# MoE of a two-layer block: the backs and gathers placed by two pairs of experts, and one small tile widened

## The chip, the cores and the metric

The kernel runs on one NeuronCore of one Trainium2 chip, as one program. The metric is the device time of one execution in microseconds (us), less is better; beside it stands one execution taken by the hardware profiler. Of the core's engines PE is the matrix engine (PEld its weight loads), DVE the vector engine, ACT the scalar engine, POOL GpSimd and SP the queue that issues most DMAs. All DMAs run on 16 DMA engines.

## The reference

Two blocks follow each other on 256 tokens of width 1024. The change touches only the mixture of experts (MoE) that stands twice in the second block, once in each layer, with 16 experts of inner width 512, two per token:

```python
def routed_moe(x, router_w, router_b, w_gate, w_up, w_down):
    xt = x.reshape(B * S, D)
    aff = jax.nn.sigmoid((xt @ router_w).astype(jnp.float32))
    sel = aff + router_b.astype(jnp.float32)
    # the best of 4 groups of 4 experts, and in it the 2 best experts
    ...
    w = jnp.take_along_axis(aff, e_idx, axis=1)
    w = w / jnp.sum(w, axis=-1, keepdims=True)
    gates = jnp.einsum('nk,nke->ne', w, jax.nn.one_hot(e_idx, N_EXPERTS, dtype=jnp.float32)).astype(x.dtype)
    y = jnp.zeros_like(xt)
    for e in range(N_EXPERTS):
        h = jax.nn.silu(xt @ w_gate[e]) * (xt @ w_up[e])
        y = y + gates[:, e:e + 1] * (h @ w_down[e])
    return y.reshape(B, S, D)
```

All of it is float32. The weights of one MoE layer are 96 pieces of 1 MB.

## The kernel before

`moe` (from line 1071) computes one MoE layer. Each expert has room for `CAP` = 64 tokens, so two experts (a pair) fill the 128 partitions, and there are `NP` = 8 pairs. A 0/1 matrix `Dg` says which token stands in which place of which expert (`places`). Four steps use it:

- `gather(q, xr)` brings the tokens of four experts (two pairs) into their places: for each of eight blocks of 128 columns four matmuls of `xr`, the high and the low half of the tokens, with `Dg` (line 1123), and an ACT eviction into `xg[q]` (line 1125). `gather(0)` stands ahead of the experts.
- `back` makes what leads back. Sixteen small matmuls (line 1132) take the gates to the places, two DVE copies put them into `gs` (lines 1134, 1135); sixteen transposes (line 1140) turn `Dg`, four ACT copies put them into `DT` (line 1142).
- `pair_in(load, j, between)` does the gate (tag A) and up (tag B) products of pair `j`, 32 matmuls `pe` (line 1154) with the two experts side by side in the array, calls `between()` after tag A, and multiplies `silu`, `gs` and the up product (line 1164).
- `flip` transposes the result (line 1170); `pair_out` does the down products `yp` (line 1185), splits them, and adds them to `x` through `DT` with the matmuls `psc` (lines 1197 to 1199).

`experts` runs `pair_in(j)`, `pair_out(j-1)`, `flip(j)` for the eight pairs. A float32 matmul stands in the trace as two instructions. The order on each engine is made by the framework's planner from this order and its own costs, so small steps are found mixed with `pe`.

The weights come through `Loads`: 96 loads of 1 MB in a fixed order on SP, which takes its DMAs in order. Each goes into a slot; `take` hands a loaded slot to the matmuls and `give` puts it back, upon which the next load is issued. The slots are opened in steps: M1 and M2 (5 together), three that are used once, M3 (6, not filled again from load 84 on), and M4 (2). M4 lies where `xr` and the router's tiles lay, so `room_left` opens it after the last gather. Two loads are issued as it opens.

`between` before: pair 0 `back` and `counts`, pair 1 `gather(1)`, pair 2 `gather(2)`, `gather(3)` and `room_left`. The counts tell whether an expert has more than 64 tokens; a loop that handles such a case (line 1350 on) follows each layer and is not entered here.

The pool `sp` holds small tiles for the whole program. Its tile `mr` is 128 x 1; a tile takes at least 32 bytes of a partition, and there are two buffers.

Of the kernel before, what the change touches and what calls it, by code (L numbers as in the profile page):

```python
# [7 lines left out]
F32 = mybir.dt.float32  # L8
# [7 lines left out]
P = 128  # L16
T = 256
NT = T // P
D = 1024
# [6 lines left out]
CAP, NP = 64, 8  # L26
# [42 lines left out]
class Net:  # L69
# [1016 lines left out]
    def moe(self, x, l, mp, load, early, mixed, probe, ahead):  # L1086
# [6 lines left out]
        nc, A, tc = self.nc, self.A, self.tc  # L1093
        v, mm = nc.vector, nc.tensor.matmul
        with ExitStack() as ctx:
            room, op = (ctx.enter_context(tc.tile_pool(name=n, bufs=1, reuse_waits="tile")) for n in ("m2", "mo"))
            gates, mask = (op.tile([P, NT, 16], F32, name=n) for n in ("gates", "mask"))
            Dg = op.tile([P, NT, 16 * CAP], F32R, name="Dg")
            DT = op.tile([P, NP, T], F32R, name="DT")
            gs, r = op.tile([P, NP], F32, name="gs"), op.tile([P, NT, 16], F32, name="r")  # L1100
# [14 lines left out]
            def gather(q, xr, tags="D"):  # L1115

                xg[q] = zone[q // 2][:, q % 2].rearrange("p (k n) -> p k n", k=KD)
                for k in range(KD):
                    if k % 2 == 0:
                        pg = self.bank(tags, "pg")  # L1120
                    ps = pg[:, T * (k % 2):T * (k % 2) + T]
                    for n, (t, a) in enumerate((t, a) for t in range(NT) for a in xr):
                        mm(ps, a[:, t, P * k:P * k + P], Dg[:, t, T * q:T * q + T], start=(n == 0),
                           stop=(n == 2 * NT - 1))
                    nc.scalar.activation(xg[q][:, k], ps, AF.Identity, bias=sh[:, k:k + 1], scale=sc[:, k:k + 1])

            def back():

                pg = self.bank("D", "pgs")
                for j in range(NP):  # L1130
                    for t in range(NT):
                        mm(pg[:, 2 * j:2 * j + 2], Dg[:, t, P * j:P * j + P].bitcast(F32), gates[:, t, 2 * j:2 * j + 2],
                           start=(t == 0), stop=(t == NT - 1))
                v.tensor_copy(gs[0:64], pg[0:64, 0:16:2])
                v.tensor_copy(gs[64:128], pg[64:128, 1:16:2])
                for j in range(0, NP, 2):
                    ps = self.bank("D", "pdt")
                    for i in range(2):
                        for t in range(NT):
                            nc.tensor.transpose(ps[:, T * i + P * t:T * i + P * t + P],  # L1140
                                                Dg[:, t, P * (j + i):P * (j + i) + P].bitcast(F32), self.ident)
                    nc.scalar.copy(DT[:, j:j + 2], ps.rearrange("p (i n) -> p i n", i=2))

            def pair_in(load, j, between=lambda: None):

                pss = []
                for tag in "AB":
                    ps = self.bank(tag, "pe")
                    for c in range(2):
                        ws = [load.take() for _ in range(2)]  # L1150
                        for k in range(4):
                            for e, (w, _) in enumerate(ws):
                                b = CAP * e
                                mm(ps[b:b + CAP], xg[j // 2][:, 4 * c + k, P * (j % 2) + b:P * (j % 2) + b + CAP],  # L1154
                                   w[:, 512 * k:512 * k + 512], start=(c == 0 and k == 0), stop=(c == 1 and k == 3),
                                   tile_position=(0, b))
                        for w in ws:
                            load.give(w)
                    pss.append(ps)
                    if tag == "A":  # L1160
                        between()
                sg = sp.tile([P, 512], F32, name="sg")
                nc.scalar.activation(sg, pss[0], AF.Silu)
                v.scalar_tensor_tensor(sg, sg, gs[:, j:j + 1], pss[1], ALU.mult, ALU.mult)  # L1164
                return sg

            def flip(sg):
                pt = self.bank("D", "pt")
                for i in range(4):
                    nc.tensor.transpose(pt[:, P * i:P * i + P], sg[:, P * i:P * i + P], self.ident)  # L1170
                hT = sp.tile([P, 4, P], F32, name="hT")
                nc.scalar.copy(hT, pt.rearrange("p (i m) -> p i m", i=4))
                return hT
# [29 lines left out]
            def experts(load, first, after):  # L1203
                prev = None
                for j in range(NP):
                    sg = pair_in(load, j, after.get(j, lambda: None))
                    if prev is not None:
                        pair_out(load, *prev)
                    prev = (j, flip(sg), ALPHA if first and j == 0 else 1.0)
                pair_out(load, *prev)  # L1210

            with ExitStack() as rt:
                rp = rt.enter_context(tc.tile_pool(name="rt", bufs=1))
                f = lambda name, shape: rp.tile(shape, F32, name=name)
                xr = [rp.tile([P, NT, D], F32R, name=n) for n in ("xrh", "xrl")]
# [8 lines left out]
                ps = self.bank("A", "cs2")  # L1224
# [6 lines left out]
                def scored(t, y):  # L1231

                    lt = lg[:, 16 * t:16 * t + 16]

                    def logits(n):
                        ps = self.bank("BD"[t], "ptr")
                        for q in range(4):
                            k = 4 * n + q
                            nc.tensor.transpose(ps[:, P * q:P * q + P], x[:, t, P * k:P * k + P], self.ident)
                        xT = rp.tile([P, 4, P], F32, name="xT", tag="xT", bufs=2)  # L1240
                        nc.scalar.copy(xT, ps.rearrange("p (q m) -> p q m", q=4))
                        for q in range(4):
                            k = 4 * n + q
                            mm(lt, xT[:, q], w2[:, 0, k], start=(k == 0), stop=(k == KD - 1))
                    self.summed(x, t, y, logits)
                    m, rs = self.moments(t)
                    z, mr = self.sp.tile([P, 16], F32, name="z", tag="z"), self.sp.tile([P, 1], F32, name="mr", tag="mr")
                    v.tensor_scalar(mr, m, rs, -1.0, ALU.mult, ALU.mult)
                    v.scalar_tensor_tensor(z, cs2[:, 0], mr, cs2[:, 1], ALU.mult, ALU.add)
                    v.scalar_tensor_tensor(z, lt, rs, z, ALU.mult, ALU.add)  # L1250
                    nc.scalar.activation(aff[:, t], z, AF.Sigmoid)
                    box.append(v.tensor_scalar(xn[t], x[:, t], m, rs, ALU.subtract, ALU.mult).ins)
# [77 lines left out]
                def counts():  # L1330
                    cn = self.bank("D", "cn")
                    mm(cn[:, 0:16], self.ones, mask[:, 0], start=True, stop=False)
                    mm(cn[:, 0:16], self.ones, mask[:, 1], start=False, stop=True)
                    v.tensor_reduce(of[:, 0:1], cn[0:1, 0:16], AX.X, ALU.max)
                    v.tensor_scalar(of[:, 1:2], of[:, 0:1], float(CAP), None, ALU.is_gt)
                    v.tensor_copy(over, of[:, 1:2])
# [3 lines left out]
                def room_left():  # L1340
                    rt.close()
                    load.open(rt.enter_context(tc.tile_pool(name="m4", bufs=1, reuse_waits="tile")), M4)
                experts(load, True, {0: lambda: (back(), counts()), 1: lambda: gather(1, xr),
                                     2: lambda: (gather(2, xr), gather(3, xr), room_left())})
            more.close()
            self.open_weights()
            first = ahead()
# [2 lines left out]
            with tc.If(left > 0):  # L1350
                with tc.tile_pool(name="r2", bufs=1) as rp:
                    xr = [rp.tile([P, NT, D], F32R, name=n) for n in ("xrh", "xrl")]
                    with tc.For_i(0, T // CAP - 1, 1):
                        for t in range(NT):
                            self.split(xr[0][:, t], xr[1][:, t], xn[t])
                        v.tensor_scalar(r, r, float(-CAP), None, ALU.add)
                        for q in range(4):
                            places(q)
                            gather(q, xr)
                        back()  # L1360
                        load = self.expert_loads(l)
                        load.open(early, M1[l])
                        load.open(room, M2[l])
                        experts(load, False, {})
        return gb, first

    def expert_loads(self, l):
# [397 lines left out]
```

## Time and profile before

| | us |
|---|---|
| median of the runs shown (3) | 2248.41 |
| lowest and highest | 2245.25, 2248.60 |
| profiled execution, its own time | 2246.95 |
| profiled execution, its span | 2244.80 |
| DVE busy in it | 1285.5 |
| ACT busy in it | 836.4 |
| PE busy in it | 2103.6 |

The span is the time between the first and the last instruction of the program in the trace; the execution's own time has some 2 us around it. PE busy counts pipelined matmuls with modelled ends, so a busy PE may still be waiting for its weights in part. The granted clock is that of the matrix engine: 1.00 is 2.4 GHz and 0.50 is 1.2 GHz. In the trace the first MoE layer lies between about 1577 and 1831 us, the second between about 1979 and 2233 us.

### The profile page before, as it was taken

How to read it: one execution, taken by the hardware profiler on the slowest of the kernel's cores; microseconds unless marked ns; L12 is line 12 of the kernel's file. 1: busy time of each engine (PE TensorE's matmuls, PEld its weight loads, DVE VectorE, ACT ScalarE, POOL GpSimd, SP SyncE). 2: the span in 40 equal slices, each digit the busy share in tenths (PEclk: the TensorE clock that was granted, in tenths of full speed). 3: DMA queues.
4: the chain of work that ended last, by engine and by line, in shares of the span. 5: the costliest groups of instructions: out<-in, count | busy, mean ns of one | idle time of the engine just before them, and what ended most of it. 6: DMA issues, size and time to landing. Idle time of an engine off the chain costs nothing. (4 is left out here: it accounts for less than half of the span.)

```text
span 2244.8 us, 30723 instructions
## 1 busy us (share of the span) xinstructions
PE 2103.6 (94%) x12156; PEld 1598.4 (71%) x12156; DVE 1285.5 (57%) x2572; ACT 836.4 (37%) x1467; POOL 65.8 (3%) x76
## 2 busy tenths in 40 slices
PE   7999999999989998999999999899999968989996
PEld 5878887886879997899897999787443338644332
DVE  5897637645578768776685655667211157641213
ACT  3222325435455444444554544364220015522000
POOL 0000000102000000000000000200000021100000
PEclk9999999999999999999999999999899989989998
DMA  8567634433248875785346554433789956278996
GB/s 322 201 239 274 242 113 152 128 117 48 76 169 311 289 267 199 283 290 204 132 169 225 199 177 169 181 113 133 286 357 420 420 225 240 93 278 334 420 419 253
DMA packets 94747, 514.47 MB, mean 229 GB/s; under 512 B 19648, under 2 KB 21056, under 8 KB 43520
## 3 DMA queue, kind: packets, MB, share of 16 engines
q1 hardware_dynamic: 88272, 502.34, 59.9%
q10 hardware_dynamic: 5168, 5.85, 0.8%
q0 software_dynamic: 1152, 4.19, 0.6%
q8 instruction: 99, 1.62, 0.3%
q14 instruction: 56, 0.46, 0.1%
HBM read 511.30 MB, written 1.05 MB: 228 GB/s over the span
## 5 line engine op out<-in xcount | busy, mean ns | idle before, releaser
L106 DVE TENSOR_TENSOR wlo<-raw,whi 128x1024 fp32r<-128x1024 f32 x421 | 514.2, 1232 | 285.4 <-ACT whi L105 282.9
L105 ACT CAST whi<-raw 128x1024 fp32r<-128x1024 f32 x421 | 434.6, 1048 | 626.6 <-PE pa L160 186.1
L160 PE MATMUL pa<-hh,whi 128*128 128x256 f32 (+1 forms) x720 | 224.0, 311 | 4.6 <-DVE hh L285 4.6
L160 PE MATMUL pa<-hl,whi 128*128 128x256 f32 (+1 forms) x720 | 223.1, 310 | 0.6 <-DVE hl L286 0.5
L160 PE MATMUL pa<-hh,wlo 128*128 128x256 f32 (+1 forms) x720 | 222.2, 309 | 0.0
L160 PE MATMUL pb<-hh,whi 128*128 128x256 f32 (+1 forms) x720 | 221.4, 308 | 0.0
L160 PE MATMUL pb<-hh,wlo 128*128 128x256 f32 (+1 forms) x720 | 221.1, 307 | 0.0
L160 PE MATMUL pb<-hl,whi 128*128 128x256 f32 (+1 forms) x720 | 220.9, 307 | 0.0
L363 DVE SCALAR_TENSOR_TENSOR macc<-rawm,cs,macc 128x512 f32<-128x512 f32 x266 | 193.2, 749 | 13.1 <-DMA rawm<-in_w_mod 9.1
L192 PE MATMUL yacc<-whi,gh 128*128 128x512 f32 x440 | 172.8, 398 | 1.3 <-ACT gate L383 1.3
L193 PE MATMUL yacc<-wlo,gh 128*128 128x512 f32 x440 | 171.6, 393 | 0.0
L1164 DVE SCALAR_TENSOR_TENSOR sg<-sg,gs,pe 128x512 f32<-128x512 f32 x16 | 12.0, 747 | 246.8 <-PE pe L1154 246.8
L160 PEld LDWEIGHTS pa<-hh,whi 128*128 128x128 f32 x720 | 138.4, 192 | 18.1 <-DVE hh L285 5.1
L160 PEld LDWEIGHTS pa<-hl,whi 128*128 128x128 f32 x720 | 138.3, 192 | 10.4 <-DVE hl L286 1.6
L1185 PE MATMUL yp<-mw,hT 128*64 128x512 f32 x512 | 138.6, 597 | 7.5 <-DMA mw<-in_w_dn 6.2
L160 PEld LDWEIGHTS pa<-hh,wlo 128*128 128x128 f32 x720 | 138.2, 192 | 6.4
L160 PEld LDWEIGHTS pb<-hh,whi 128*128 128x128 f32 x720 | 136.7, 190 | 6.2
L160 PEld LDWEIGHTS pb<-hl,whi 128*128 128x128 f32 x720 | 136.7, 190 | 6.2
L195 PE MATMUL yacc<-whi,gl 128*128 128x512 f32 x440 | 141.0, 394 | 0.0
L160 PEld LDWEIGHTS pb<-hh,wlo 128*128 128x128 f32 x720 | 136.3, 189 | 6.2
L1154 PE MATMUL pe<-mw,xgH 128*64 128x512 f32 x512 | 122.2, 597 | 8.0 <-DMA mw<-in_w_gu 8.0
L1154 PE MATMUL pe<-mw,xgY 128*64 128x512 f32 x464 | 126.1, 608 | 0.0
(469 smaller groups left out, 3706.8 us busy)
## 6 DMA issues: line engine op xcount, KB each, us to landing
mw<-in_w_gu SPq DMA_DIRECT2D x122, 1024.0 KB, 17.2
raw<-in_ffn_w_in SPq DMA_DIRECT2D x88, 1024.0 KB, 5.0
rawm<-in_w_mod SPq DMA_DIRECT2D x72, 1024.0 KB, 5.8
mw<-in_w_dn SPq DMA_DIRECT2D x64, 1024.0 KB, 15.7
raw<-in_ffn_w_out SPq DMA_DIRECT2D x55, 1024.0 KB, 5.1
raw<-in_mix_wT SPq DMA_DIRECT2D x8, 1024.0 KB, 5.1
raw<-in_sg_wR SPq DMA_DIRECT2D x8, 1024.0 KB, 5.1
raw<-in_sg_wT SPq DMA_DIRECT2D x8, 1024.0 KB, 4.9
```

The lines of the kernel that those rows point to most:

```text
L105: self.nc.scalar.copy(hi, src)
L106: self.nc.vector.tensor_tensor(lo, src, hi.bitcast(F32), ALU.subtract)
L160: self.nc.tensor.matmul(o, w[:, k], h[:, k], start=(k == 0 and i == 0), stop=(k == nk - 1 and i == len(steps) - 1))
L192: mm(y[n], a, whi[:, cs[n]], start=first, stop=False)
L193: mm(y[n], a, wlo[:, cs[n]], start=False, stop=False)
L195: mm(y[n], b, whi[:, cs[n]], start=False, stop=last)
L363: v.scalar_tensor_tensor(o, raw[:, k], w, o, ALU.mult, ALU.add)
L1154: mm(ps[b:b + CAP], xg[j // 2][:, 4 * c + k, P * (j % 2) + b:P * (j % 2) + b + CAP], w[:, 512 * k:512 * k + 512], start=(c == 0 and k == 0 ...
L1164: v.scalar_tensor_tensor(sg, sg, gs[:, j:j + 1], pss[1], ALU.mult, ALU.mult)
L1185: mm(yp[n][b:b + CAP], hT[:, i, b:b + CAP], w[:, D * k + 512 * n:D * k + 512 * n + 512], start=(i == 0), stop=(i == 3), tile_position=(0, b))
```

## The change

`back` becomes `back(j)` and does the gates and the transposes of two pairs, j and j+1. `between` becomes one function of j: the even pairs call `back(j)` (pair 0 also `counts`), pairs 1, 3 and 5 call `gather(1)`, `gather(2)` and `gather(3)`, and `room_left` stands in pair 5, after `gather(3)`. `gather(1)` and the counts stay where they were. The loop that is not entered calls `back` in four parts. The tile `mr` is made 128 x 16, of which the first column is used; two buffers of it take 64 bytes each instead of 32.

```diff
@@ -1124,22 +1124,21 @@
                            stop=(n == 2 * NT - 1))
                     nc.scalar.activation(xg[q][:, k], ps, AF.Identity, bias=sh[:, k:k + 1], scale=sc[:, k:k + 1])
 
-            def back():
-
-                pg = self.bank("D", "pgs")
-                for j in range(NP):
+            def back(j):
+
+                pg, ps = self.bank("D", "pgs"), self.bank("D", "pdt")
+                for i in range(2):
                     for t in range(NT):
-                        mm(pg[:, 2 * j:2 * j + 2], Dg[:, t, P * j:P * j + P].bitcast(F32), gates[:, t, 2 * j:2 * j + 2],
-                           start=(t == 0), stop=(t == NT - 1))
-                v.tensor_copy(gs[0:64], pg[0:64, 0:16:2])
-                v.tensor_copy(gs[64:128], pg[64:128, 1:16:2])
-                for j in range(0, NP, 2):
-                    ps = self.bank("D", "pdt")
-                    for i in range(2):
-                        for t in range(NT):
-                            nc.tensor.transpose(ps[:, T * i + P * t:T * i + P * t + P],
-                                                Dg[:, t, P * (j + i):P * (j + i) + P].bitcast(F32), self.ident)
-                    nc.scalar.copy(DT[:, j:j + 2], ps.rearrange("p (i n) -> p i n", i=2))
+                        mm(pg[:, 2 * i:2 * i + 2], Dg[:, t, P * (j + i):P * (j + i) + P].bitcast(F32),
+                           gates[:, t, 2 * (j + i):2 * (j + i) + 2], start=(t == 0), stop=(t == NT - 1))
+                for e in range(2):
+                    b = slice(CAP * e, CAP * e + CAP)
+                    v.tensor_copy(gs[b, j:j + 2], pg[b, e:4:2])
+                for i in range(2):
+                    for t in range(NT):
+                        nc.tensor.transpose(ps[:, T * i + P * t:T * i + P * t + P],
+                                            Dg[:, t, P * (j + i):P * (j + i) + P].bitcast(F32), self.ident)
+                nc.scalar.copy(DT[:, j:j + 2], ps.rearrange("p (i n) -> p i n", i=2))
 
             def pair_in(load, j, between=lambda: None):
 
@@ -1203,7 +1202,7 @@
             def experts(load, first, after):
                 prev = None
                 for j in range(NP):
-                    sg = pair_in(load, j, after.get(j, lambda: None))
+                    sg = pair_in(load, j, lambda: after(j))
                     if prev is not None:
                         pair_out(load, *prev)
                     prev = (j, flip(sg), ALPHA if first and j == 0 else 1.0)
@@ -1244,7 +1243,7 @@
                             mm(lt, xT[:, q], w2[:, 0, k], start=(k == 0), stop=(k == KD - 1))
                     self.summed(x, t, y, logits)
                     m, rs = self.moments(t)
-                    z, mr = self.sp.tile([P, 16], F32, name="z", tag="z"), self.sp.tile([P, 1], F32, name="mr", tag="mr")
+                    z, mr = self.sp.tile([P, 16], F32, name="z", tag="z"), self.sp.tile([P, 16], F32, name="mr", tag="mr")[:, 0:1]
                     v.tensor_scalar(mr, m, rs, -1.0, ALU.mult, ALU.mult)
                     v.scalar_tensor_tensor(z, cs2[:, 0], mr, cs2[:, 1], ALU.mult, ALU.add)
                     v.scalar_tensor_tensor(z, lt, rs, z, ALU.mult, ALU.add)
@@ -1340,8 +1339,16 @@
                 def room_left():
                     rt.close()
                     load.open(rt.enter_context(tc.tile_pool(name="m4", bufs=1, reuse_waits="tile")), M4)
-                experts(load, True, {0: lambda: (back(), counts()), 1: lambda: gather(1, xr),
-                                     2: lambda: (gather(2, xr), gather(3, xr), room_left())})
+                def between(j):
+                    if j % 2 == 0:
+                        back(j)
+                    elif j < NP - 1:
+                        gather(j // 2 + 1, xr)
+                    if j == 0:
+                        counts()
+                    if j == NP - 3:
+                        room_left()
+                experts(load, True, between)
             more.close()
             self.open_weights()
             first = ahead()
@@ -1357,11 +1364,12 @@
                         for q in range(4):
                             places(q)
                             gather(q, xr)
-                        back()
+                        for j in range(0, NP, 2):
+                            back(j)
                         load = self.expert_loads(l)
                         load.open(early, M1[l])
                         load.open(room, M2[l])
-                        experts(load, False, {})
+                        experts(load, False, lambda j: None)
         return gb, first
 
     def expert_loads(self, l):
```

## Rows read from the trace of the kernel before

**Rows 1.** The page's 40 slices: PE busy, GB/s moved.
```profile
PE   7999999999989998999999999899999968989996
...
GB/s 322 201 239 274 242 113 152 128 117 48 76 169 311 289 267 199 283 290 204 132 169 225 199 177 169 181 113 133 286 357 420 420 225 240 93 278 334 420 419 253
```

**Rows 2.** Windows, layer 0, flip to flip: span; PE, PEld, DVE, ACT, POOL; clock; DMA; GB/s.
```profile
1609.70:1641.60 31.90, 31.89 (x144) 12.67 (x144) 4.70 (x7) 6.49 (x12) 0.00 (x0) 1.00 0.89 358
1641.60:1677.90 36.30, 36.30 (x175) 16.11 (x173) 4.70 (x7) 10.63 (x20) 0.00 (x0) 1.00 0.79 322
1677.90:1701.30 23.40, 23.08 (x103) 8.09 (x101) 4.10 (x7) 2.36 (x4) 0.00 (x0) 1.00 1.01 419
1701.30:1727.10 25.80, 25.52 (x108) 9.00 (x108) 4.53 (x8) 2.36 (x4) 0.00 (x0) 1.00 1.01 421
1727.10:1757.10 30.00, 27.28 (x109) 9.28 (x109) 4.68 (x8) 2.36 (x4) 0.00 (x0) 1.00 1.01 419
```

**Rows 3.** The same windows in layer 1, pair 5.
```profile
2129.10:2159.00 29.90, 27.22 (x109) 9.26 (x109) 4.61 (x8) 2.36 (x4) 0.00 (x0) 1.00 1.01 420
```

**Rows 4.** Windows by the state of the weight stream, both layers.
```profile
1585.00:1668.00 83.00, 82.82 (x407) 37.01 (x406) 7.55 (x15) 21.15 (x39) 0.73 (x2) 0.98 0.74 292
1601.00:1608.00 7.00, 7.00 (x38) 2.96 (x38) 0.45 (x3) 1.07 (x2) 0.00 (x0) 1.00 0.00 0
1658.00:1664.00 6.00, 6.00 (x36) 3.61 (x36) 0.00 (x0) 2.78 (x6) 0.00 (x0) 1.00 0.01 3
1664.00:1668.00 4.00, 4.00 (x22) 1.30 (x19) 0.75 (x1) 0.32 (x1) 0.00 (x0) 1.00 0.82 287
1668.00:1818.00 150.00, 139.96 (x572) 48.12 (x568) 26.99 (x41) 13.50 (x23) 0.00 (x0) 1.00 1.01 420
1998.50:2006.50 8.00, 8.00 (x30) 3.06 (x30) 0.44 (x3) 1.80 (x4) 0.00 (x0) 0.72 0.01 2
2059.50:2065.50 6.00, 6.00 (x36) 3.41 (x32) 0.00 (x0) 2.67 (x6) 0.00 (x0) 1.00 0.00 0
```

**Rows 5.** SP's waits, 1580 to 1820: waited for, total us, times, longest.
```profile
SPq L50 <- PE pe L1154: 96.0, 34, 20.0
...
SPq L50 <- PE pg L1123: 15.6, 1, 15.6
```

**Rows 6.** PE's timeline in pair 0: start, us, instruction, count.
```profile
1592.42 3.73 PE L1132 MATMUL pgs<-gates,Dg 128*128 128x2 f32 x32
1596.02 1.69 PE L1140 MATMUL pdt<-ident,Dg 128*128 128x128 f32 x8
1597.64 3.17 PE L1154 MATMUL pe<-xgH,xgY 128*64 128x512 f32 x6
1600.74 1.09 PE L1140 MATMUL pdt<-ident,Dg 128*128 128x128 f32 x8
1601.77 1.08 PE L1154 MATMUL pe<-xgH,xgY 128*64 128x512 f32 x4
...
1603.33 1.08 PE L1154 MATMUL pe<-xgH,xgY 128*64 128x512 f32 x4
```

**Rows 7.** A window just after the gate matmuls of pair 0.
```profile
1598.00:1600.00 2.00, 2.00 (x5) 0.46 (x2) 0.00 (x0) 0.34 (x1) 0.00 (x0) 0.50 1.00 422
```

**Rows 8.** PE's timeline, the down products of pairs 2 and 3.
```profile
1690.09 7.45 PE L1185 MATMUL yp<-mw,hT 128*64 128x512 f32 x31
...
1715.21 8.21 PE L1185 MATMUL yp<-mw,hT 128*64 128x512 f32 x31
```

**Rows 9.** Page, DMA issues: KB each, median us to landing.
```profile
mw<-in_w_gu SPq DMA_DIRECT2D x122, 1024.0 KB, 17.2
```

**Rows 10.** Line 1142, the copy out of the transposes: ns min/median/max.
```profile
L1142 ACT CAST DT<-pdt x8: 586/586/592, 1596.7 to 2003.8; 128x512 fp32r<-128x512 f32 x8
```

**Rows 11.** Groups of line 106 at two places: busy us, mean ns.
```profile
L106 DVE TENSOR_TENSOR Y<-o,Y 128x256 fp32r<-128x256 f32 x16 | 6.8, 424 | 10.5 <-ACT Y L105 10.5
...
L106 DVE TENSOR_TENSOR sgl<-x,sgh 128x256 fp32r<-128x256 f32 x16 | 6.7, 423 | 2.5 <-ACT sgh L105 2.5
```

## The prediction

> **What bounds the kernel now.** I read the slices first, to find where the weight stream runs [rows 1]. Slices 31 and 32, 38 and 39 of the 40 move about 420 GB/s: the later parts of the two MoE layers. PE shows 8 and 9 there too, so its busy digit cannot say which of the two is waited for. That is read from the windows cut at the start of `flip` of one pair and of the next [rows 2]. Pairs 3, 4 and 5 run the same program, without gather or back, in 23.4, 25.8 and 30.0 us, and pairs 6 and 7 repeat the 30.0 of pair 5. In all of them DMA is at 1.01. Pairs 1 and 2 have gathers, take 31.9 and 36.3 us, and DMA is at 0.89 and 0.79. So each MoE layer has two halves. In the first PE is the slower one and the stream starves for slots; in the second the stream is full and PE waits for weights. Layer 1 repeats this [rows 3].
>
> How much does PE wait in the second half? The 31 matmuls of line 1185 took 7.45 us in the window of pair 3 and 8.21 in that of pair 4 [rows 8]; pair 4 without these 0.8 us of waiting is 25.0, say 25.1 with the small change of what stands before either flip. Pair 3's 23.4 is no base, since PE did part of its matmuls before the flip of pair 2. Three pairs at 29.9 therefore hold 3 x 4.8 us of waiting, and with 0.8 in pair 4 this makes **15.2 us per layer that PE could get back**.
>
> How much does the stream lose in the first half? From 1585 to 1668 it ran at 292 GB/s, from 1668 to 1818 at 420 [rows 4]: 83 x (1 - 292/420) = 25.3 us of stream time lost. Two holes stand out: 1601 to 1608 at 0 GB/s, and 1658 to 1664 at 3, with 287 GB/s in the 4 us behind it; in layer 1 1998.5 to 2006.5 and 2059.5 to 2065.5. The waits of SP's queue name their causes [rows 5]: up to 20.0 us behind pe (line 1154), and once 15.6 us behind pg (line 1123). The first is pair 0, where PE does the whole `back` before the tile that comes free next is used up. The second is the `room_left` of pair 2: SP takes its DMAs in order, the first load into M4 needs the room of `xr`, so it waits for gather 3, and loads whose slots were long free queue behind it.
>
> **The change part by part.** *Back, pair 0.* From 1592.42 to 1603.33 PE did 32 gate matmul instructions (3.7 us), 16 of the transposes (1.7 and 1.1), the counts (0.6), and ten pe instructions [rows 6]. At the full clock a pe takes 0.214 us, as the 32 of yp in rows 8 do (7.45 less 0.6 for the end of the last), ten 2.1. So back and counts cost 10.9 - 2.1 = 8.8 us. In them are 1.9 us because six pe took 3.17 instead of 1.3 [rows 6]: the granted clock was 0.50 there, the 1.2 GHz level [rows 7]. `back(0)` has a quarter of the gate matmuls and half of the transposes: 8 x 3.73/32 = 0.9, and 8 transposes at 1.1, with 0.1 for the switches 2.1 us. With counts 2.7 instead of 8.8: pair 0 ends 6.1 us earlier and its late slots come back 6.1 us earlier.
>
> *Back, pairs 2, 4 and 6.* Each adds 2.1 us on PE, two copies on DVE and one of 0.59 us on ACT [rows 10], engines that are busy for 4.1 to 4.5 and 2.4 us of such a pair [rows 2]. Over the layer PE does 4 x 2.1 + 0.6 = 9.0 instead of 8.8 us: plus 0.2. (The diff transposes every pair once as before; 4 x 4 instead of 16.) From below: with no switches and no half clock 1.9; from above what the whole back cost before, 8.2. I take 2.1, since the rows of the same instructions give it.
>
> *New waits.* The product of line 1164 for pairs 2, 4, 6 needs `gs` from `back(j)`. Both copies stand ahead of it on DVE's own queue, and half a pair of pe lies between. The psc matmuls need `DT`, through ACT, and a whole pair_out lies between. Pair 4 waits for gather 2, now half a pair ahead instead of a pair and a half. The eight evictions of a gather fit between the pe of tag B and yp (pair 1 already works so, and its gather was half a pair ahead as well). All three at nothing; if the cover failed, one ACT copy of 0.6 us per back.
>
> *Gathers 2 and 3.* Their PE work moves from pair 2 to pairs 3 and 5, unchanged. Pair 1 tells the price: 31.9 against 25.1, of which at most 0.4 are other matmuls, so 6 or more; pair 2 with two is 36.3, so 5.6 each. A pair with one gather is about 31 us, which is the pace of the stream (12 loads at 2.5 us are 30). What ACT gets with it (6.5 instead of 2.4 us, pairs 1 and 3) stays hidden.
>
> *M4.* `room_left` issues two loads on SP's queue; they now stand behind the returns of pairs 2 to 4 and of tag A of pair 5. The 15.6 us wait of pair 2 goes, and with it the hole: 6.0 us at nothing and 4 x (1 - 287/420) = 1.3 behind it, **7.3 us of stream**. What it costs: between pairs 2 and 5 there are 11 slots instead of 13. A load takes 17.2 us to land in the median [rows 9], at 2.5 us each some 7 in flight, and PE holds two to four. So 11 just do.
> In pair 5 SP waits again, for one gather instead of two: about half of 15.6. Seven loads in flight are 17 us of stream and outlast it. I take nothing and keep 7.3 us per layer for the rivals.
>
> *The padded tile.* It moves what the program places above pool `sp` on the left side by 64 bytes. No row shows a cost of such a place: the same split of 128 x 256 took 423 ns into tiles that start at 96 and 424 into tiles that start at 224 mod 256 [rows 11]. Zero; that they differ by 0.2% bounds it to 1 us either way, an estimate.
> The Trainium skill, DMA: Bandwidth & Descriptors, section How a descriptor splits into AXI transactions, says that a transfer which doesn't start at a multiple of 256 bytes needs one transaction more; by this layout only M4's two slots get there (192 to 0), for which an estimate is 24 loads x 2.5/33 = 1.8 us per layer. No run here shows a large load into such a place; by that rule the time would be 2217, and the sum does without it.
>
> **The sum.** Stream: 6.1 + 7.3 = 13.4 us per layer come back. PE: 15.2 us of waiting less 0.2 could be saved. The smaller counts, 13.4, and PE then still waits for 1 to 2 us; the next limits lie close together. What comes behind a layer (norms, the next mixer) hangs on its last product and moves along. Two layers: 27 us (26.8). The profiled execution took 2246.95 us with a span of 2244.8; it would be 2220. It lies 1.5 us below the median 2248.41 of the runs shown, so the median becomes 2221.
>
> **The rivals.** *Half clock at each back.* If each of the four backs brings the clock to 0.50 as the one did, each costs 1.9 more for pe and 0.6 for its transposes (1.69 against 1.09), about 4.6 in all: 18.4 + 0.6 - 8.8 = 10.2 more on PE, which leaves 5.0 per layer: 2238. For it: the rows show that dip right behind gate matmuls and transposes. Against it: they were 48 instructions in a row, now 16, and each flip with its transposes and psc passes at 1.00 [rows 2].
> *Slower: a back has a fixed price.* If what back cost is not its instructions but the change between kinds of work, the emptying of the two banks of tag D and the clock, then a quarter costs as much as the whole: 4 x 8.2 + 0.6 - 8.8 = 24.6 us more on PE per layer against 15.2 of waiting, 9.4 slower per layer: 2267. It decides from (8.8 + 15.2 - 0.6)/4 = 5.9 us per back. Against it: 7.1 of the 8.8 us are instructions in the rows.
> *The hole moves.* M4's loads hold SP in pair 5 as in pair 2, or 11 slots are too few and the stream starves in pairs 3 to 5: only the 6.1 of pair 0 remain per layer, 2236.
> *It doesn't do what it says.* The planner orders PE's queue by its own costs; if it draws the backs and gathers to where they were, nothing moves: 2248.
>
> **How the numbers follow.** Forecast 2221 with chance 0.65 (own range 2211 to 2230, for a back between 1.9 and 3 and the two limits that nearly meet); half clock 0.13; the hole moves 0.10; nothing moves 0.05; slower 0.07. The range 2211 to 2238 takes in the forecast, the moved hole and half of the clock's case. This kernel can be told from no change from about 0.2% on, 4.5 us. Faster: 0.65 + 0.13 + 0.10, less a margin for what no case names, 0.84; same 0.07; slower 0.09.
>
> **What would show it.** In the profile after: pair 0 6 us shorter with a smaller hole near 1601; no SP wait of 15 us behind pg, one of under 10 in pair 5; DMA at 1.0 from pair 2 on; pairs 5 to 7 near 27 us or less; gs copies four times per layer. Wrong: clock of 0.50 behind each back, more than 4 us of PE per back, or DMA below 0.9 in pairs 3 to 5.

## The result, and the profile after

| | median us | own time of the profiled execution |
|---|---|---|
| before | 2248.51 | 2246.95 |
| after | 2208.40 | 2213.07 |

The ratio of after to before is 0.9825, with an interval of 0.9803 to 0.9847: 40 us faster. 2221 was forecast, with a range of 2211 to 2238. The direction was right, the time lies below the range.

Where the two profiled executions part can be read from the starts in PE's timeline. (An FFN is a feed-forward network; three of them over all 256 tokens stand ahead of the MoE layers. In their products `hh` and `hl` are the high and the low half of the tokens' values, `whi` and `wlo` those of the weights.) All 33.9 us between them (2246.95 - 2213.07) are in this table:

| stretch | before | after | gain |
|---|---|---|---|
| start to the first `pa<-hh,whi` of the FFNs over 256 tokens | 669.2 | 674.3 | -5.1 |
| from there to the first `pe` of layer 0 | 913.4 | 896.8 | 16.6 |
| first `pe` to the last `psc` of layer 0 | 246.0 | 235.1 | 10.9 |
| to the first `pe` of layer 1 | 154.8 | 155.5 | -0.7 |
| layer 1, likewise | 247.1 | 234.9 | 12.2 |

The loss of 5.1 us stands in the context stages that the diff doesn't touch; it is of this one execution, which took 4.7 us more than after's median. `pad_only`, below, comes to that place at 669.5. The gain of 16.6 us stands in stages of which the prediction said nothing but "zero". Some 3 us of it are of this one trace of before: five kernels below whose operands there stand in the same places mod 256 as before's take 909.5 to 910.5 us for the stretch, not 913.4. The two MoE layers gained 23.1 where 27 were forecast.

First the MoE layers. After's page, slices, GB/s:

```profile
GB/s 319 195 241 276 265 113 135 131 116 71 58 164 248 300 308 172 286 334 242 103 173 248 172 189 192 155 125 134 300 399 418 421 220 257 96 273 400 417 420 220
```

Against [rows 1] the stream now has about 400 GB/s or more in three slices of a layer, before it had 420 in two. The windows of after from flip to flip in layer 0, as [rows 2] (span; PE, PEld, DVE, ACT, POOL; granted clock; DMA share; GB/s):

```profile
1591.76:1623.70 31.94, 31.94 (x146) 12.70 (x145) 4.70 (x7) 6.48 (x12) 0.00 (x0) 1.00 0.90 359
1623.70:1648.78 25.08, 24.77 (x115) 9.66 (x113) 4.38 (x9) 2.94 (x5) 0.00 (x0) 1.00 1.01 420
1648.78:1682.19 33.41, 32.37 (x140) 13.04 (x141) 4.61 (x8) 6.53 (x12) 0.00 (x0) 1.00 1.01 415
1682.19:1709.10 26.91, 26.59 (x120) 10.66 (x121) 4.93 (x10) 2.94 (x5) 0.00 (x0) 1.00 1.01 420
1709.10:1742.53 33.43, 32.40 (x140) 13.06 (x140) 4.61 (x8) 6.53 (x12) 0.00 (x0) 1.00 1.01 421
1742.53:1769.44 26.91, 26.59 (x121) 10.66 (x121) 4.92 (x10) 2.94 (x5) 0.00 (x0) 1.00 1.01 421
1769.44:1794.41 24.97, 23.91 (x106) 8.40 (x106) 4.60 (x8) 2.36 (x4) 0.00 (x0) 1.00 0.88 359
```

The reader is to see three things. DMA is at 1.01 from pair 2 to pair 6, so the hole of [rows 4] near 1660 is gone. Pairs 4, 6 and 7 take 26.9, 26.9 and 25.0 us, less than the 29.9 at which the stream delivers a pair. And pairs 3 and 5, which now have the gathers, take 33.4, not the 31 that the prediction gave them. What PE waited for between the first and the last of these flips, first before (us in total, times, longest), then after:

```profile
PE pe L1154 <- DMA mw<-in_w_gu: 4.0, 3, 1.4
PE yp L1185 <- DMA mw<-in_w_dn: 3.1, 6, 0.6
...
```

```profile
PE pt L1169 <- DVE x L1198: 1.8, 6, 0.3
PE pg L1123 <- ACT xgH L1125: 1.5, 4, 0.5
PE psc L1196 <- DVE x L1198: 0.8, 1, 0.8
```

No row of after names a DMA: PE waits for no weights any more. SP's waits in layer 0 of after, which answer to [rows 5], show who waits now:

```profile
SPq L50 <- PE pe L1153: 162.5, 47, 20.0
SPq L50 <- PE yp L1184: 28.3, 17, 2.6
...
SPq L50 <- PE pg L1123: 3.7, 3, 2.2
```

The 15.6 us behind `pg` are 3.7 in three waits, and SP stands behind PE's `pe` for 162 us instead of 96: the stream waits for PE through the whole layer. The bound has changed sides.

Pair 0 of after, PE's timeline (start, us, instruction, count), as [rows 6]:

```profile
1580.95 1.05 PE L1132 MATMUL pgs<-gates,Dg 128*128 128x2 f32 x8
1581.86 0.63 PE L1139 MATMUL pdt<-ident,Dg 128*128 128x128 f32 x4
1582.52 0.37 PE L1331 MATMUL cn<-mask,ones 128*128 128x16 f32 x2
1582.73 0.37 PE L1332 MATMUL cn<-mask,ones 128*128 128x16 f32 x2
1583.04 0.65 PE L1153 MATMUL pe<-xgH,xgY 128*64 128x512 f32 x2
```

Back and counts end 2.1 us after they begin, and the clock stays at 1.00 through every window above, and from 1577 to 1592 us, in pair 0. From the first `pe` to the flip of pair 0 it is 20.7 us where it was 27.1.

### The profile page after: what moved, and what is told of

Read it like the earlier page. It is cut to its first block, busy times and chain, and to the rows that moved or that the text cites. A ratio compares the mean times of both kernels' runs of the same rounds, so it can differ in the third digit from the quotient of the medians.

```text
span 2211.0 us, 30709 instructions
## 1 busy us (share of the span) xinstructions
PE 2078.8 (94%) x12156; PEld 1583.3 (72%) x12156; DVE 1285.6 (58%) x2584; ACT 836.9 (38%) x1467; POOL 66.5 (3%) x76
## 5 line engine op out<-in xcount | busy, mean ns | idle before, releaser
L363 DVE SCALAR_TENSOR_TENSOR macc<-rawm,cs,macc 128x512 f32<-128x512 f32 x266 | 193.3, 750 | 13.4 <-DMA rawm<-in_w_mod 9.0
L1184 PE MATMUL yp<-mw,hT 128*64 128x512 f32 x512 | 119.8, 593 | 1.4 <-ACT hT L1171 1.4
```

What stands on the lines that cost most here:

```text
L363: v.scalar_tensor_tensor(o, raw[:, k], w, o, ALU.mult, ALU.add)
L1184: mm(yp[n][b:b + CAP], hT[:, i, b:b + CAP], w[:, D * k + 512 * n:D * k + 512 * n + 512], start=(i == 0), stop=(i == 3), tile_position=(0, b))
```

## The experiments

Each was timed against the kernel before on the same chip, whose medians there were 2245.1 to 2246.2.

| run | what it is | median us | ratio to before, interval |
|---|---|---|---|
| pad_only | before, left side + 64 bytes | 2232.02 | 0.9936 (0.9917 to 0.9956) |
| move_only | after without the padded tile | 2224.44 | 0.9908 (0.9895 to 0.9920) |
| pad_128 | before, left side + 128 | 2244.11 | 0.9990 (0.9981 to 1.0000) |
| pad_256 | before, left side + 256 | 2245.20 | 0.9999 (0.9990 to 1.0008) |
| pad_192 | before, left side + 192 | 2239.11 | 0.9971 (0.9962 to 0.9980) |
| left_32 | before, left side + 32 | 2242.35 | 0.9981 (0.9970 to 0.9992) |
| right_64 | before, right side - 64 | 2228.85 | 0.9916 (0.9901 to 0.9930) |
| both_64 | before, left + 64 and right - 64 | 2244.20 | 0.9989 (0.9979 to 1.0000) |
| back_only | before, backs spread | 2239.01 | 0.9966 (0.9953 to 0.9978) |
| gath_only | before, gathers and M4 spread | 2226.90 | 0.9909 (0.9895 to 0.9924) |
| m4_only | before, M4 opened in pair 5 | 2241.69 | 0.9980 (0.9968 to 0.9991) |
| gath_late | after, gathers held behind tag A | 2199.74 | 0.9796 (0.9780 to 0.9812) |

### The two halves of the change

`pad_only` is before with the one line of the padded tile, `move_only` is after without it.

```
-self.sp.tile([P, 1], F32, name="mr", tag="mr")
+self.sp.tile([P, 16], F32, name="mr", tag="mr")[:, 0:1]
```

> Only the padded tile; the order of the MoE layers is that of before. Theory A (addresses): the 64 bytes move hh, hl, H, Y and the weight slots on the left side, and the matmuls of 256 columns that read them follow each other in 113 to 115 ns instead of 119 to 120 (line 160 in the three FFNs, lines 173 to 175 of the mixer between 1450 and 1560 us). Then 11 to 18 us go, all of them between 690 us and the first MoE layer: 2231 to 2237, and the MoE layers take what they took before, flip to flip. Rival B (my prediction): the padding does nothing, 2248 within 1 us, and the 12 us that after gained ahead of its first MoE layer come from something else, such as other phases of the granted clock.

> The new order of gates, ways back and gathers without the padded tile. Theory A: all of the MoE gain and nothing else, 22 us (10.8 and 11.5 us per layer in the two traces): 2226, and line 160 at 119 ns as before. Rival B (the padding does nothing): all of the gain, 2208. Rival C (M4's slots at 192 mod 256 are what cost): the MoE gain is smaller than in after, 2230 or more.

The padding alone takes 0.64% off, about 14 us, and the move alone 0.92%, about 21. Their product is 0.9845, inside the interval of after. In the trace of `pad_only` the MoE layers take 245.2 and 246.4 us, as before, and the stretch from the first `pa<-hh` to the first `pe` 894.0 instead of 913.4. Against the 909.5 to 910.5 of the other kernels that is 16 us. Theory A holds, and the prediction's zero for the padding falls.

### What the 64 bytes do

By the program's layout, `hh` and `hl` stand at 96, `H` and `Y` at 224 mod 256 before, `whi` and `wlo` on the right side at 224. Two lines tell the operands apart. In line 160 `hh` moves through the array (256 columns) and `whi` stands in it; in line 173 `whi` moves and `hh` or `H` stands. Three kernels shift the left side by other amounts (`[P, 24]`, `[P, 32]` and `[P, 40]` in the line above), `left_32` puts a tile of 32 bytes ahead of it, `right_64` moves the right side alone, and `both_64` moves both.

```
+self.nc.vector.memset(pool("rp", 1, side="right").tile([P, 16], F32, name="rpad"), 0.0)
 self.ws = ctx.enter_context(ExitStack())
 self.open_weights()
```

> Before with the tile padded further, so that the left side moves by 128 bytes (hh and hl from 96 to 224 mod 256, H and Y and the left weight slots from 224 to 96). Theory A as a rule of the distance between an operand and the others: the time lies elsewhere than with 64 bytes; if each step of 64 bytes helps alike, 2215 to 2225; if what counts is that H and Y and the right-side weights no longer stand at the same 224, about 2231 to 2237 as with 64; if what counts is hh at 160, back to 2248. Rival B: 2248 in any case.

> Before with the left side moved by 256 bytes: every address mod 256 is that of before. Theory A with a rule mod 256: 2248 within 3 us, line 160 at 119 ns. If 64 bytes help here as well because another modulus (512, 1024) or the absolute place counts, it differs from 2248 by 5 us or more. Rival B: 2248.

> Before with one tile of 32 bytes ahead of the left side: hh and hl at 128, H, Y and the left weight slots at 0 mod 256, the right side at 224. By theory R the distance hh to whi is 96 mod 128 here, against 0 before (and with 128 bytes, both slow) and 64 with the padded tile (fast). If the gain grows with the distance from 0, this lies between, 2238 or so; if only a whole 64 bytes count it is 2245; if places at whole multiples of 128 or 256 are the best for themselves, it is below the 2232 of the padded tile.

> Before with the right side of the memory (the tiles raw, whi and wlo of the stages with 256 tokens, M3's slots) moved down by 64 bytes, to 160 mod 256; the left side, with hh and hl at 96 and H and Y at 224, stays. Theory R (what counts is how the place of the stationary operand lies to that of the moving one): line 160 is as fast as with the left side moved, 113 to 115 ns a matmul, and the time is that of the padded tile alone, 2229 to 2235. Theory S (the place of hh, H and Y by itself counts): they have not moved, line 160 stays at 119 ns, and the time is 2245. Theory W (the place of the weights by itself counts): it would have to be read as R, since whi moved; with the padded tile whi had not moved, which speaks against W already.

> Before with the left side moved by 192 bytes: hh and hl at 32, H and Y at 160 mod 256, the right side at 224. By theory R the distance from the moving to the stationary operand is +64 here where the padded tile makes it -64: line 160 at 113 to 114 ns and 2229 to 2235. If the sign matters, it lies between that and 2245. If the place of the left operand by itself counted, this place would be a new one and say nothing; right_64 has answered that.

> Before with the padded tile and with the right side moved down by 64 bytes: hh and hl at 160, whi and wlo at 160, H and Y at 32 mod 256. Each of the two alone gave 13 to 18 us. So far the rows read: with the moving operand 64 bytes below the stationary one (mod 256) a matmul of line 160 takes 113 to 114 ns, 64 above 118, at the same place 120, 128 apart 119. Here hh and whi stand at the same place, so line 160 must go back to 120 ns and the time to 2243 to 2247. If each of the two moves helps for itself, it is 2215 to 2220; if only one of them counts, 2229 to 2232.

The rows of line 160 in the second FFN over 256 tokens, from 900 us on (duration min/median/max in ns, first and last start), of before, `pad_only`, `right_64`, `pad_192` and `both_64` in this order (the added line makes 160 to 161 in two of them):

```profile
L160 PE MATMUL pa<-hh,whi x152: 279/282/287, 900.8 to 1060.1; 128*128 128x256 f32 x152
```

```profile
L160 PE MATMUL pa<-hh,whi x144: 276/276/285, 902.4 to 1050.2; 128*128 128x256 f32 x144
```

```profile
L161 PE MATMUL pa<-hh,whi x149: 276/276/285, 899.9 to 1052.8; 128*128 128x256 f32 x149
```

```profile
L160 PE MATMUL pa<-hh,whi x148: 278/280/282, 900.0 to 1055.7; 128*128 128x256 f32 x148
```

```profile
L161 PE MATMUL pa<-hh,whi x150: 277/283/283, 899.7 to 1057.2; 128*128 128x256 f32 x150
```

It is the median that speaks, not the maximum. The records overlap, and what the time is made of is the step from one start to the next: its median over line 160 in these FFNs is 119 ns in before, 113 in `pad_only`, 113 to 114 in `right_64`, 118 in `pad_192` and 120 in `both_64`. `right_64` left `hh` where it was and has the 276 of `pad_only`: theory S falls. `both_64` has `hh` where `pad_only` has it and `whi` where `right_64` has it, and is at 283: the two moves cancel, to the time of before. What counts in these rows is the distance between the operands. `pad_192` shows that it has a sign, since line 173 turns the two roles round. Before, then `pad_192`:

```profile
L173 PE MATMUL pv<-whi,hh x124: 278/281/1053, 1084.0 to 1129.7; 128*128 128x256 f32 x124
L173 PE MATMUL pv<-whi,H x32: 283/283/283, 1494.4 to 1505.5; 128*128 128x256 f32 x32
```

```profile
L173 PE MATMUL pv<-whi,hh x109: 276/276/276, 1084.8 to 1121.5; 128*128 128x256 f32 x109
L173 PE MATMUL pv<-whi,H x32: 280/280/282, 1484.6 to 1495.6; 128*128 128x256 f32 x32
```

With `hh` at 32, the same `hh` and `whi` give 280 ns where `hh` moves and 276 where it stands. All kernels in one table: the place of the moving operand less that of the stationary one, mod 256, then the median of the row; last the time from the first `pa<-hh` to the first `pe` in the timelines.

| run | line 160, hh moves | line 173, H stands | line 173, hh stands | stretch, us |
|---|---|---|---|---|
| before | 128: 282 | 0: 283 | 128: 281 | 913.4 |
| pad_256 | 128: 282 | 0: 283 | 128: 281 | 910.1 |
| pad_128 | 0: 283 | 128: 281 | 0: 283 | 912.2 |
| both_64 | 0: 283 | 128: 281 | 0: 283 | 911.2 |
| left_32 | 160: 281 | 224: 280 | 96: 281 | 909.7 |
| pad_192 | 64: 280 | 64: 280 | 192: 276 | 903.3 |
| pad_only | 192: 276 | 192: 276 | 64: 279 | 894.0 |
| right_64 | 192: 276 | 192: 276 | 64: 280 | 892.7 |
| after | 192: 276 | 192: 276 | 64: 279 | 896.8 |

In these rows a distance gives the same duration within 1 ns in every kernel and both lines: 283 at 0, 281 to 282 at 96, 128 and 160, 279 to 280 at 64 and 224, 276 at 192. Of the last column only the 903.3 of `pad_192` and the three rows near 895 stand out; the others lie at or within the 909.5 to 913.4 of the kernels with the places of before.

The distance is not the whole rule. By the layout `pu` of line 160 stands at the same 192 in `pad_only`, in the stage that follows, but is at 281, as it was before:

```profile
L160 PE MATMUL pu<-hh,whi x128: 276/281/369, 1118.4 to 1170.7; 128*128 128x256 f32 x128
```

In the first FFN of `right_64`, too, the median of `pa<-hh,whi` is 281, at 192. So at 192 a matmul takes 276 or 281; what decides between the two no run shows.

The size fits: from the first to the last `pa<-hh,whi` the first two of these FFNs take 390.9 us in before and 380.7 in `pad_only`, the third 175.7 and 170.3. That is 15.6 us in three times 1056 matmuls of line 160 (six rows of 176), 5 ns each, and it is nearly all of the 16 us above. Why the chip does this no run shows.

### The parts of the move

`back_only` spreads the backs and leaves gathers and M4; `gath_only` spreads gathers and M4 and does all four backs in pair 0; `m4_only` is before with one step changed:

```
-1: lambda: gather(1, xr), 2: lambda: (gather(2, xr), gather(3, xr), room_left())
+1: lambda: gather(1, xr), 2: lambda: (gather(2, xr), gather(3, xr)), 5: room_left
```

> No padded tile. The backs are spread over pairs 0, 2, 4 and 6; the gathers and the opening of M4 stand where they stood before, in pairs 1 and 2. By my prediction's sum pair 0 alone gives 6.1 us of stream per layer: 2245.6 - 12 = 2233. Rival: what holds the second half is the hole behind M4's loads in pair 2, and whatever pair 0 saves is waited for there: 2243 or more.

> No padded tile. All four backs in pair 0 as before; gathers in pairs 1, 3 and 5, M4 opened in pair 5. By my prediction's sum the hole in pair 2 gives 7.3 us of stream per layer: 2245.6 - 15 = 2231, while pair 0 keeps its wait. With the rival reading (PE is the bound, and each gather in pairs 3 and 5 costs 2 to 3 us more of PE than it did in pair 2) the sum is 7.3 less what PE can't hide: if PE no longer waits for weights at all, 2234 to 2238. The two parts together gave 21 us; if they add without a second limit, back_only and gath_only sum up to 27.

> Before with one change: M4 is opened in pair 5, not behind the gathers of pair 2; gathers and back stand where they stood. No padded tile. Theory H (my prediction: the hole at pair 2 is SP's queue standing behind M4's first load): the hole goes, 7.3 us of stream per layer, 2231. Since the two gathers of pair 2 are the cheap ones (5.6 us each), it can even be below gath_only: down to 2224. Rival L: while PE does the two gathers it gives back no slots, and with 11 instead of 13 of them the stream stands still there for the same time: 2240 or more.

`gath_only` has all of the move's gain, 0.9909 against 0.9908 of `move_only`; `back_only` has 0.34%, and it doesn't add. Both expectations for `gath_only` were missed: 2226.90 is below the 2231 and below the 2234 to 2238. `back_only` lies between its two. Windows of `back_only`, pairs 2, 4 and 5:

```profile
1632.04:1670.16 38.12, 38.10 (x186) 17.36 (x184) 5.01 (x9) 11.29 (x21) 0.00 (x0) 1.00 0.72 294
...
1693.57:1720.48 26.91, 26.60 (x121) 10.67 (x121) 4.92 (x10) 2.94 (x5) 0.00 (x0) 1.00 1.01 420
1720.48:1750.15 29.67, 27.09 (x108) 9.34 (x108) 4.60 (x8) 2.35 (x4) 0.00 (x0) 1.00 1.01 420
```

Pair 0 gave 6.3 us, where 6.1 were forecast (first `pe` to flip 20.9). Pair 2 took 1.9 back for its own back, pair 4 another 1.0, and pair 5 waits for the stream as it did. With the hole of pair 2 still there 3.6 us are left of layer 0 and 5.1 of layer 1. Windows of `gath_only`, pairs 4, 6 and 7:

```profile
1693.87:1718.99 25.12, 24.81 (x108) 8.67 (x108) 4.61 (x8) 2.35 (x4) 0.00 (x0) 1.00 1.01 420
...
1752.42:1777.54 25.12, 24.80 (x109) 8.66 (x109) 4.61 (x8) 2.35 (x4) 0.00 (x0) 1.00 1.01 418
1777.54:1803.62 26.08, 25.00 (x107) 8.66 (x107) 4.61 (x8) 2.35 (x4) 0.00 (x0) 1.00 1.01 420
```

With the gathers spread PE hardly waits for weights (1.1 us in pair 7). Then a back costs its 1.8 us of PE (pair 4: 26.91 in after, 25.12 here) wherever it stands: four in pair 0, or one in each of four pairs, is nearly the same sum: the layers take 235.8 and 237.2 us in `gath_only`, 235.7 and 234.9 in `move_only`. This is why the spread backs add next to nothing.

`m4_only` gained 0.20%, 4.5 us, where 15 were expected by theory H. Its windows of pairs 2 and 3:

```profile
1639.26:1675.49 36.23, 36.23 (x174) 16.06 (x172) 4.70 (x7) 10.63 (x20) 0.00 (x0) 1.00 0.91 365
1675.49:1698.90 23.41, 23.10 (x103) 8.10 (x101) 4.07 (x7) 2.36 (x4) 0.00 (x0) 1.00 0.99 401
```

SP's waits that touch pair 2 of `m4_only` (window 1639 to 1680):

```profile
SPq L50 <- PE pe L1154: 33.2, 10, 8.2
```

Before, the same pair shows 15.6 us behind `pg` and 15.6 behind `pe`. Now SP no longer stands behind `pg`, and pair 2 moves 365 GB/s instead of 322: 36.2 x 43/420 = 3.7 us of stream. But it stays below 420 and pair 3 falls to 401, 1 us lost. PE is still in its two gathers and gives back no slots, and with 11 of them SP stands behind `pe` instead: 33.2 us, about the two waits of before together. What is left, 2.7, is about what layer 0 gained (2.4, first `pe` to last `psc`) and layer 1 (2.3). So rival L holds: the wait of 15.6 us had the name of SP's order, but behind it lay a PE that did two gathers in a row.

### A gather in pieces

In after the planner put the gathers of pairs 3 and 5 right behind the flip, in pieces. PE's timeline in pair 3 of after (idle time and its cause in brackets):

```profile
1648.78 0.66 PE L1169 MATMUL pt<-ident,sg 128*128 128x128 f32 x4 [0.31 <-DVE x L1198]
...
1649.93 3.65 PE L1153 MATMUL pe<-mw,xgY 128*64 128x512 f32 x14
...
1654.17 1.07 PE L1153 MATMUL pe<-mw,xgY 128*64 128x512 f32 x2
...
1656.56 0.38 PE L1123 MATMUL pg<-Dg,xrh 128*128 128x256 f32 x1 [0.54 <-ACT xgH L1125]
...
1658.27 3.65 PE L1153 MATMUL pe<-mw,xgY 128*64 128x512 f32 x14
...
1662.87 1.07 PE L1153 MATMUL pe<-mw,xgY 128*64 128x512 f32 x2
```

The gather's 32 instructions lie in pieces of 3, 4, 14, 7 and 4 between these `pe`. `gath_late` holds them behind the last product of tag A:

```
-                        gather(j // 2 + 1, xr)
+                        with tc.issue_after(i.ins):      # i: last pe of tag A
+                            gather(j // 2 + 1, xr)
```

> After with one change: the gathers of pairs 1, 3 and 5 are held behind the last product of tag A of their pair, so that they stand in blocks of 8 and 16 matmuls between full pe, as pair 1 has them, and not in pieces of 3, 4, 14, 7 and 4 right behind the flip. Theory G (PE is the bound of the MoE layers in after, and pieces make a gather dearer, 8.4 against 6.9 us): pairs 3 and 5 take 31.9 instead of 33.4 us and the time falls by 4 x 1.5 = 6 us against after, 2202. Rival (the weight stream is the bound, PE's pieces fill time in which it would wait): 2208 as after.

Its windows of pairs 3 and 5:

```profile
1643.17:1674.42 31.25, 30.74 (x141) 12.69 (x141) 4.61 (x8) 6.47 (x12) 0.00 (x0) 1.00 1.01 419
...
1701.33:1732.55 31.22, 30.72 (x141) 12.68 (x141) 4.61 (x8) 6.48 (x12) 0.00 (x0) 1.00 1.01 421
```

33.4 became 31.2, in blocks of 8, 16 and 8. Four such pairs give 8.8 us. The median is 2199.74, against 2208.40 of after in its own comparison; by the two ratios to before it is 6.5 us. 6 were expected. The two intervals still overlap (0.9780 to 0.9812 and 0.9803 to 0.9847), so it is the windows that carry this reading, more than the medians. This kernel is the fastest of all, 2.04% below before. Of the 2.2 us per pair 0.5 are PE's waits for ACT's copies of the gather (0.73 to 0.19 in pair 3); 1.0 lies in the changes between `pg` and `pe`, by the starts in the two timelines: four steps from `pe` to `pg` and five back, 3.24 us together, became three and three, 2.19. The rest lies mostly in the steps from one `pe` to the next (13.6 and 13.1 us); why they are longer in after is open. Nothing new is late: in this kernel too no wait of PE between the flips names a DMA.

## Why the prediction was wrong

*What bounds the kernel*: right. PE could get back 15.2 us per layer, it said. `gath_late`, in which PE waits for no weights, takes 230.5 and 230.6 us from first `pe` to last `psc`, 15.5 and 16.5 less than before.

*Back*: right in size, with one slip. 2.1 us per back were forecast, pairs 4 and 6 show 26.9 - 25.1 = 1.8 (against the same pairs of `gath_only`). It counted eight transposes per back, half of 16, where the diff makes four. Pair 0 came 6.5 us earlier, 6.1 were forecast, and the copies into `gs` and `DT` are named in no wait of PE between the flips. But in the sum the 6.1 us were worth next to nothing: `gath_only`, without them, has the whole gain of the move.

*The clock*: the rival of a dip behind each back fell, all windows are at 1.00. The rival of a fixed price per back, 8.2 us each, fell too: a back costs 1.8.

*M4*: the wait went, as forecast. But the step that gave it a price was wrong in its cause: the 7.3 us were put down to SP's order of DMAs, with M4 late as the cure. `m4_only` shows that M4 late alone is worth 2.3 to 2.4 us per layer. The cure is one gather per pair. The rival of the moved hole fell: SP waits behind `pg` 3.7 us in all, and 11 slots kept the stream at 1.01.

*Gathers*: this is the mis-sized term of the MoE sum. The prediction took 5.6 to 6 us for each and called a pair with one about 31. Pairs 3 and 5 took 33.4: 8.4 each over the 25.0 of pair 7. The gathers were taken as unchanged because the instructions were; the planner placed them otherwise. This is also where the "new waits" at nothing were too cheap: `pg` waits for ACT, 1.5 us in layer 0, where before it did not.

*The sum*: min(13.4, 15.0) took the stream as the limit. It was PE: from pair 2 to pair 6 PE waited for no weights, while SP stood behind `pe`. Nor was 13.4 the stream's limit, since `gath_late` gained more than that; it priced two holes, of the 25.3 us that the prediction itself found lost in the first half. The layers gained 10.9 and 12.2, and with the dear gathers mended 15.5 and 16.5, which is the PE term of the sum. So the MoE part fell 4 us short of 27 because the dear gathers took 8.8 from a PE term that was worth 32 in two layers.

*The padded tile*: here the prediction failed, and this alone put the time below the range. It took "zero, within 1 us" from the row of a DVE operation [rows 11], though the tiles that moved are read by PE, and though it itself showed that nearly every slice is PE's. No pair of matmul rows was looked at. The trace of before held one: line 173, 283 ns with `H` and 281 with `hh`, the same form at two distances. It would not have given the 276, but it would have been a hint that PE is not blind to the place. In place of zero the padding alone measured 14 us (`pad_only`), by shorter steps of the matmuls that read the moved tiles. No rival gave it a price on PE.

*M4 at 0 mod 256*: the prediction said that no run showed a large load into such a place; now several do. By their layout two of the 13 slots stand at 0 in `pad_only`, five in `left_32`, none before. In pair 6, where the stream is the bound, the windows are 29.78, 29.71 and, before, 29.94 us: 0.16 and 0.23 less. The Trainium skill, DMA: Bandwidth & Descriptors, How a descriptor splits into AXI transactions, says that a transfer which starts off a multiple of 256 bytes needs one transaction more; one less in 33 is an estimate of 0.14 and 0.35 us per pair. By that rule, the traces agree in sign. The size they do not settle: `pad_128`, `pad_192` and `right_64`, with no slot at 0, show 29.84 to 29.89, and `both_64`, with two, 29.71. The prediction's 24 loads per layer were a miscount: by the layout 12 of a layer's 96 loads go into M4 before, 6 in after, so its estimate of 1.8 us becomes 0.5. In after PE is the bound, and its pairs 2 to 7 take what they take in `move_only`, where M4 is not at 0. The windows, `pad_only` and then `left_32`:

```profile
1737.53:1767.31 29.78, 27.23 (x108) 9.25 (x109) 4.61 (x8) 2.36 (x4) 0.00 (x0) 1.00 1.01 421
```

```profile
1756.21:1785.92 29.71, 27.16 (x108) 9.30 (x108) 4.60 (x8) 2.35 (x4) 0.00 (x0) 1.00 1.01 422
```

## What to carry to other kernels

A change that moves a tile's address is a change to every engine that reads that tile: price it by rows of that engine, and time it alone, as that one line was a third of the gain here. A wait named for a queue's order may only show where its head happens to stand; ask what the releaser was doing, and whether the next wait has the same cause. Where PE no longer waits for weights, a shorter path on PE is what helped next (`gath_late`), and moved work is to be priced at the place where the planner puts it.

## What the runs showed of the hardware

- In lines 160 and 173 the duration of a matmul of 256 columns in fp32r goes with the place of its moving operand less that of its stationary one in a partition, mod 256: 276 ns at 192, 279 to 280 at 64, 281 to 282 at 128, 283 at 0 (medians of the rows in the table). It is the difference, not either place (`right_64`, `both_64`), and has a sign (`pad_192`); a shift by 256 changed no row (`pad_256`). At 192 some matmuls stay at 281 (`pu` in `pad_only`); what decides that is open, and so is the cause of the whole.
- Shifting one side of the memory by 64 bytes, no work changed, was worth 0.64% (left side up, `pad_only`) or 0.84% (right side down, `right_64`) of the whole kernel; shifting both by these amounts (`both_64`) 0.11%, with an interval that reaches no change.
